# Spreading the block transfers of a head's transposition over eight steps in a two-layer decoder kernel

## The chip, the cores and the metric

The kernel runs on one core of a Trainium2 chip. The metric is the time of one execution on the device in microseconds (us); lower is better. The core has five engines that run side by side and wait for each other through semaphores: TensorE (PE in the rows, its weight loads PEld), VectorE (DVE), ScalarE (ACT), GpSimd (POOL) and SyncE (SP), which here only issues DMA transfers. Each engine works through its own list of instructions in order.

## The reference

The input x has 256 positions of 2048 numbers. Two layers follow, each with a norm, one wide projection, a mixer over 32 heads of 128, a gate and a projection back.

```
def even_layer(x, norm_g, w_in, q_gain, k_gain, w_out):
    hdn = rms_norm(x, norm_g)
    proj = jnp.einsum('bsd,de->bse', hdn, w_in)
    qa, ka, va, qb, kb, vb, gate = split_cols(
        proj, [D_SB, D_SB, D_SB, D_DIL, D_DIL, D_DIL, D_INNER])
    oa = stick_breaking_attention(to_heads(qa), to_heads(ka), to_heads(va))
    ob = dilated_attention(to_heads(qb), to_heads(kb), to_heads(vb), q_gain, k_gain)
    mix = jnp.concatenate([oa.reshape(b, s_len, D_SB), ob.reshape(b, s_len, D_DIL)], axis=-1)
    mix = mix * jax.nn.silu(gate.astype(jnp.float32))
    return x + jnp.einsum('bse,ed->bsd', mix.astype(x.dtype), w_out)

def odd_layer(x, norm_g, w_in, lb, o_gain, w_out):
    hdn = rms_norm(x, norm_g)
    proj = jnp.einsum('bsd,de->bse', hdn, w_in)
    q, f_pre, inp, gate = split_cols(proj, [D_INNER, D_INNER, D_INNER, D_INNER])
    o = hgrn2(to_heads(q), to_heads(f_pre), to_heads(inp), lb)
    o = rms_norm(o, o_gain).reshape(b, s_len, D_INNER)
    mix = o * jax.nn.silu(gate.astype(jnp.float32))
    return x + jnp.einsum('bse,ed->bsd', mix.astype(x.dtype), w_out)
```

Heads 0 to 15 of the first layer are stick-breaking attention, heads 16 to 31 a mixture of three dilated causal softmax attentions, and the 32 heads of the second layer are HGRN2, a gated linear recurrence.

## The kernel before

**Steps.** The wide projection runs head by head: 16 *steps* a head, each one block of 128 input channels times 512 columns (128 each of q, k or forget gate, v, and gate). A step is six matmuls of 128x512 (`product`, lines 277 to 279): the single-precision product is made from a rounded part and a rest of each factor, hi x hi, hi x lo and lo x hi, for two halves of the sequence. Each layer ends with an output projection of 4 x 32 such steps. All in all there are 1280 steps.

**Weights.** `Feed` brings in 512 KB for two steps at a time: a load on SP's queue (L223, tile `raw`, four buffers), a rounding copy on ACT (L234, `whi`) and a subtraction on DVE (L235, `wlo`), together called a *split* here. `take` keeps four splits ahead, and `whi` and `wlo` have four buffers each, so the split for a pair of steps can only begin when PE has finished the pair four pairs before.

**Side work.** When a head's 16 steps are done, its generator (`head`) is added to `Side`. After every step of what follows, `tick` advances each generator whose count has run out; `yield n` means that the rest is written n steps later. So the work of head h is written between the matmuls of the next heads: `evacuate` (L300) copies q and k into `qkp` and v and gate into `pj`, then comes the gate, the transposition of q and k (`turn_pair`), the products (L336, L337 for attention; L487 and after for HGRN2), the softmax or its like, its transposition (`flip_weights`, L137), the product with the values (L327 to L329), and the mix, which is transposed again (`emit_mix`, L137) and split for the output projection. The order in which the instructions of each engine finally stand is set by a list scheduler of the framework, which may move work by a part of a step or a few.

**The transposition.** VectorE can transpose blocks of 32x32 only, so the blocks are first carried to their places by 16 DMA transfers of 16 KB, all on SP's queue (`move_blocks`, L148, from `qkp` to `mvp`). `yield 4` later one DVE instruction turns them in place (`turn_blocks`, L155). The last head of a layer is transposed on PE instead (`quick`). SP's queue also carries all weight loads.

**The three kinds.** Stick-breaking: transfers 2 steps after the evacuation, turn 4 later, products 3 later. Dilated: transfers 5 after the evacuation, since q and k need their norms first, turn 4 later together with a scaling of k on ACT (L385), products 3 later. HGRN2: transfers 2 after, turn 4 later, then a chain of some 20 small DVE operations from the forget gate (L431 to L480, most of them recorded under the helper's line L439), and 10 steps later the first scores on PE (L487): two matmuls from tile `sp`, then two that read `qv`, the last tile of that chain.

Of the kernel before, what the change touches and what calls it, by code (L numbers as in the profile page):

```python
# [10 lines left out]
F32 = mybir.dt.float32  # L11
# [7 lines left out]
P = 128  # L19
D = 2048  # L20
SEQ = 256
NT = SEQ // P
NKT = D // P
NH = 32
# [4 lines left out]
LB_FLOOR = 2.0 ** -28  # L29
GATE_FLOOR = -87.0  # L30
AHEAD = 4


@with_exitstack
def hybrid_trunk(
# [21 lines left out]
    work = ctx.enter_context(tc.tile_pool(name="work", bufs=3))  # L57
# [27 lines left out]
    def constants():  # L85

        nc.sync.dma_start(ident, eye)
        nc.sync.dma_start(strict, cmask[:, 2, :])
        nc.sync.dma_start(bias, cmask[:, 0, :])
        nc.sync.dma_start(hg, headg)  # L90
        nc.sync.dma_start(lbr, lbl)
        nc.sync.dma_start(mult, cmask[:, 1, :])
        hmf = work.tile([P, 4, 80], F32, name="pj", bufs=2)
        nc.sync.dma_start(hmf, hmask)
        yield 1
        nc.vector.scalar_tensor_tensor(
            qkg, hg[:, 0:1], 1.0 / math.sqrt(P), hg[:, 1:2], op0=ALU.mult, op1=ALU.mult
        )
        yield 1
        for t in range(NT):  # L100
            nc.vector.tensor_copy(hm[:, 4 * t : 4 * t + 4, :], hmf)

        nc.vector.tensor_max(lbm, lbr[:, 0, :], lbr[:, 1, :])
        for j in range(2):
            nc.vector.tensor_sub(lbe[:, j, :], lbr[:, j, :], lbm)
        nc.scalar.activation(lbe, lbe, AF.Exp)
        nc.vector.tensor_add(lbs, lbe[:, 0, :], lbe[:, 1, :])
        nc.vector.reciprocal(lbs, lbs)
        nc.vector.tensor_mul(lb, lbe[:, 1, :], lbs)
        nc.vector.tensor_scalar(oml, lb, -1.0, 1.0, op0=ALU.mult, op1=ALU.add)  # L110
        nc.vector.tensor_scalar_max(lbc, lb, LB_FLOOR)
# [21 lines left out]
    def flip(blocks):  # L133

        ps = psb.tile([P, len(blocks) * P], F32, name="att")
        for i, b in enumerate(blocks):
            nc.tensor.transpose(ps[:, i * P : (i + 1) * P], b, ident)  # L137
        return ps

    def move_blocks(src, name):  # L140

        n = src.shape[2] // P
        moved = work.tile([P, NT, n, 4, 32], F32, name=name, bufs=1)
        to = moved.rearrange("p t c a j -> p (t c) a j")
        v = src.rearrange("p t (c f) -> p (t c) f", f=P)
        for a in range(4):
            for b in range(4):
                nc.sync.dma_start(  # L148
                    to[32 * b : 32 * b + 32, :, a, :], v[32 * a : 32 * a + 32, :, 32 * b : 32 * b + 32]
                )  # L150
        return moved

    def turn_blocks(dst, moved):

        nc.vector.transpose(dst, moved.rearrange("p t c a j -> p (t c a j)"))  # L155

    def turn_pair(qk, quick):


        if quick:  # L160
            ps = flip([qk[:, t, c * P : (c + 1) * P] for t in range(NT) for c in range(2)])
            nc.scalar.copy(qk, ps.rearrange("p (t f) -> p t f", t=NT))
        else:
            moved = move_blocks(qk, "mvp")
            yield 4
            turn_blocks(qk.rearrange("p t f -> p (t f)"), moved)

    def flip_weights(w):

        ps = flip([w[:, j * P : (j + 1) * P] for j in range(3)])  # L170
        at = work.tile([P, 384], F32, name="atk", bufs=2)
        nc.scalar.copy(at, ps)
        return at
# [37 lines left out]
    class Feed:  # L211
# [26 lines left out]
        def take(self):  # L238
            while len(self.parts) < AHEAD:
                n = len(self.parts)  # L240
                self.split()
                if len(self.parts) == n:
                    break
            return self.parts.pop(0)
# [49 lines left out]

    def evacuate(acc, rstd):
        qk = work.tile([P, NT, 256], F32, name="qkp", bufs=2)
        vg = work.tile([P, NT, 256], F32, name="pj", bufs=2)
        for dst, c in ((qk, 0), (vg, 256)):
            for t in range(NT):
                nc.scalar.activation(  # L300
                    dst[:, t, :], acc[t][:, c : c + 256], AF.Copy, scale=rstd[:, t : t + 1]
                )
        return qk, vg

    def gate_exp(vg):

        g = vg[:, :, P:]
        sg = work.tile([P, NT, P], F32, name="sg")
        nc.vector.tensor_scalar(sg, g, GATE_FLOOR, -1.0, op0=ALU.max, op1=ALU.mult)
        nc.scalar.activation(sg, sg, AF.Exp)  # L310
        nc.vector.tensor_scalar_add(sg, sg, 1.0)
        nc.vector.reciprocal(sg, sg)  # L312
        nc.vector.tensor_mul(sg, sg, g)
        return sg
# [3 lines left out]
    def emit_mix(h, mix, scale):  # L318
        mixed.append(h)
        split_into(mixh[:, h, :], mixl[:, h, :], flip([mix[:, t, :] for t in range(NT)]), scale)  # L320
# [18 lines left out]

    def stick_breaking(h, qk, vg):  # L340
        sg = gate_exp(vg)
        yield 2
        yield from turn_pair(qk, False)
        yield 3
        zp = products(qk)
        z = work.tile([P, 384], F32, name="wt", bufs=2)
        nc.vector.scalar_tensor_tensor(
            z, zp, 1.0 / math.sqrt(P), strict, op0=ALU.mult, op1=ALU.add
        )
        sp = work.tile([P, 384], F32, name="qv", bufs=2)  # L350
        nc.scalar.activation(sp, z, AF.Abs)
        nc.scalar.activation(sp, sp, AF.Exp, scale=-1.0)
        nc.scalar.activation(sp, sp, AF.Ln, bias=1.0)
        nc.vector.scalar_tensor_tensor(sp, z, 0.0, sp, op0=ALU.max, op1=ALU.add)

        for lo, hi in ((0, 128), (128, 384)):
            back = sp[:, lo:hi][:, ::-1]
            nc.vector.tensor_tensor_scan(back, one.broadcast_to([P, hi - lo]), back, 0.0, ALU.mult, ALU.add)
        nc.vector.tensor_sub(z, z, sp)
        nc.scalar.activation(z, z, AF.Exp)  # L360
        yield 12
        at = flip_weights(z)
        yield 3
        o = weighted_values(at[:, 0:128], at[:, 128:256], at[:, 256:384], vg)
        nc.vector.tensor_mul(sg, o, sg)
        yield 2
        emit_mix(h, sg, 1.0)

    def dilated(h, qk, vg):
        sg = gate_exp(vg)  # L370
# [8 lines left out]
        for t in range(NT):  # L379
            sl = qk[:, t, P:]  # L380
            nc.vector.tensor_scalar_mul(sl, sl, rr[:, 2 * t + 1 : 2 * t + 2])
        yield 5
        yield from turn_pair(qk, h == NH - 1)
        k = qk[:, :, P:]
        nc.scalar.activation(k, k, AF.Copy, scale=qkg)  # L385
        yield 3
        z = products(qk)
        nm = small.tile([P, NT], F32, name="nm")
        ws = small.tile([P, NT], F32, name="ws")
# [30 lines left out]

    def hgrn(h, qk, vg):
        g = vg[:, :, P:]
        sg = work.tile([P, NT, P], F32, name="sg")
        nc.scalar.activation(sg, g, AF.Sigmoid)
        nc.vector.tensor_mul(sg, sg, g)
        yield 2
        yield from turn_pair(qk, h == NH - 1)
        q, fp = qk[:, :, 0:P], qk[:, :, P:]
        fk = work.tile([P, 2, SEQ], F32, name="qk", bufs=2)
# [188 lines left out]
    for layer in range(2):  # L618
        for h in range(NH):
            acc = accumulators()  # L620
            steps = product(feed, xh, xl, NKT, acc, layer)
            for k in range(NKT):
# [4 lines left out]
                if layer == 0 and h == 0 and k % 4 == 3:  # L627
                    n = k // 4
# [98 lines left out]
```

## Time and profile before

| what | value |
|---|---|
| time, median of 3 runs | 1991.98 us (1991.17 to 1992.28) |
| the profiled execution | 1995.66 us, its span 1993.9 us |
| PE busy | 1945.4 us, 98% of the span |
| DVE busy, ACT busy | 1319.1 us (66%), 1010.2 us (51%) |
| granted clock of TensorE, mean | 0.999 |
| DMA moved | 360.79 MB, 181 GB/s |

The span reaches from the first to the last instruction of the profiled execution. A row of a timeline gives start, duration, engine, line, operation and tiles, and in brackets the time that the engine sat idle before it with the instruction that ended the wait. A matmul's shown duration overlaps that of the next one, so the distance of two starts is what one costs when they follow each other. SPq is SP's queue of DMA issues: its durations are those of issuing, not of the transfer.

### The profile page before, as it was taken

How to read it: one execution, taken by the hardware profiler on the slowest of the kernel's cores; microseconds unless marked ns; L12 is line 12 of the kernel's file. 1: busy time of each engine (PE TensorE's matmuls, PEld its weight loads, DVE VectorE, ACT ScalarE, POOL GpSimd, SP SyncE). 2: the span in 40 equal slices, each digit the busy share in tenths (PEclk: the TensorE clock that was granted, in tenths of full speed). 3: DMA queues.
4: the chain of work that ended last, by engine and by line, in shares of the span. 5: the costliest groups of instructions: out<-in, count | busy, mean ns of one | idle time of the engine just before them, and what ended most of it. 6: DMA issues, size and time to landing. Idle time of an engine off the chain costs nothing.

```text
span 1993.9 us, 26825 instructions
## 1 busy us (share of the span) xinstructions
PE 1945.4 (98%) x9032; PEld 1587.2 (80%) x9032; DVE 1319.1 (66%) x2518; ACT 1010.2 (51%) x1719; POOL 53.3 (3%) x54
## 2 busy tenths in 40 slices
PE   8999999999999999999999999999999999999999
PEld 7778877877777777888877778787877777778887
DVE  6666666666666666555557777777777777777443
ACT  6455555544444444444455555555555555555432
POOL 0000000000000000000000000000000000000000
PEclk9999999999999999999999999999999999999999
DMA  8566655655555555665555555555556555565664
GB/s 304 164 199 194 186 180 181 189 169 181 166 171 182 182 168 177 201 190 190 189 168 172 179 178 177 168 171 169 171 178 180 171 165 169 172 178 171 200 201 138
DMA packets 240267, 360.79 MB, mean 181 GB/s; under 512 B 153984, under 2 KB 155136, under 8 KB 240128
## 3 DMA queue, kind: packets, MB, share of 16 engines
q1 hardware_dynamic: 239984, 359.05, 57.9%
q8 instruction: 71, 1.16, 0.2%
q14 instruction: 68, 0.56, 0.1%
q10 hardware_dynamic: 144, 0.02, 0.0%
HBM read 340.61 MB, written 2.10 MB: 172 GB/s over the span
## 4 chain that ended last, share of the span: by engine, by line
PE 55%; DVE 18%; SPq 10%; issue 7%; ACT 5%; DMA 4%; POOL 1%; DVEq 0%; ACTq 0%; POOLq 0%
PE acc L277 17%; PE acc L279 17%; PE acc L278 17%; SPq L148 10%; DVE wlo L235 5%; ACT whi L234 4%; DMA raw<-in_w_even 2%; DVE qk L439 2%; DVE ri L455 2%; PE att L487 1%; DMA mvp<-qkp 1%; PE att L516 1%; POOL ro L202 1%; DVE sg L312 1%; DVE wt L469 1%
## 5 line engine op out<-in xcount | busy, mean ns | idle before, releaser
L235 DVE TENSOR_TENSOR wlo<-raw,whi 128x1024 fp32r<-128x1024 f32 (+1 forms) x642 | 781.3, 1218 | 447.6 <-ACT whi L234 447.1
L234 ACT CAST whi<-raw 128x1024 fp32r<-128x1024 f32 (+1 forms) x642 | 672.3, 1048 | 786.2 <-PE acc L279 654.6
L277 PE MATMUL acc<-whi,xh 128*128 128x512 f32 x2048 | 829.6, 405 | 6.1 <-ACT whi L234 6.1
L278 PE MATMUL acc<-wlo,xh 128*128 128x512 f32 x2048 | 803.9, 393 | 0.6 <-DVE wlo L235 0.6
L279 PE MATMUL acc<-whi,xl 128*128 128x512 f32 x2048 | 802.9, 392 | 0.0
L279 PEld LDWEIGHTS acc<-whi,xl 128*128 128x128 f32 x2048 | 385.5, 188 | 83.7
L277 PEld LDWEIGHTS acc<-whi,xh 128*128 128x128 f32 x2048 | 385.9, 188 | 81.8 <-ACT whi L234 6.1
L278 PEld LDWEIGHTS acc<-wlo,xh 128*128 128x128 f32 x2048 | 386.4, 189 | 74.9 <-DVE wlo L235 1.8
L277 PE MATMUL acc<-whi,mixh 128*128 128x512 f32 x512 | 202.0, 394 | 0.0
L279 PE MATMUL acc<-whi,mixl 128*128 128x512 f32 x512 | 199.5, 390 | 0.0
L278 PE MATMUL acc<-wlo,mixh 128*128 128x512 f32 x512 | 199.4, 390 | 0.0
L279 PEld LDWEIGHTS acc<-whi,mixl 128*128 128x128 f32 x512 | 96.1, 188 | 20.0
L277 PEld LDWEIGHTS acc<-whi,mixh 128*128 128x128 f32 x512 | 96.1, 188 | 19.6
L278 PEld LDWEIGHTS acc<-wlo,mixh 128*128 128x128 f32 x512 | 96.2, 188 | 19.3
L155 DVE STREAM_TRANSPOSE qkp<-mvp 128x512 f32<-128x512 f32 x62 | 44.1, 711 | 49.7 <-DMA mvp<-qkp 49.6
L300 ACT ACTIVATE qkp<-acc,rstd 128x256 f32<-128x256 f32 x128 | 60.4, 474 | 12.3 <-PE acc L279 9.3
L300 ACT ACTIVATE pj<-acc,rstd 128x256 f32<-128x256 f32 x128 | 60.2, 472 | 0.0
L312 DVE RECIPROCAL sg<-sg 128x256 f32<-128x256 f32 x32 | 56.0, 1749 | 0.5
L202 POOL TENSOR_TENSOR rr<-rv,mhalf 128x4 f32<-128x4 f32 x16 | 29.4, 1839 | 736.5 <-DVE rv L201 736.5
L439 DVE TENSOR_TENSOR qk<-qk,tots 128x128 f32<-128x128 f32 x64 | 18.5, 288 | 43.0 <-PE att L516 42.9
L202 POOL TENSOR_TENSOR ro<-rv,mhalf 128x2 f32<-128x2 f32 x32 | 22.3, 697 | 839.0 <-DVE rv L201 839.0
L558 DVE SCALAR_TENSOR_TENSOR sg<-att,ro,sg 128x128 f32<-128x128 f32 x64 | 22.1, 349 | 27.8 <-POOL ro L202 27.8
(137 smaller groups left out, 1261.1 us busy)
## 6 DMA issues: line engine op xcount, KB each, us to landing
raw<-in_w_odd SPq DMA_DIRECT2D x256, 512.0 KB, 4.6
raw<-in_w_even SPq DMA_DIRECT2D x254, 512.0 KB, 4.2
raw<-in_w_out SPq DMA_DIRECT2D x128, 512.0 KB, 3.5
mvp<-qkp SPq DMA_DIRECT2D x992, 16.0 KB, 2.1
xres<-in_xt SPq DMA_DIRECT2D x8, 256.0 KB, 6.5
xres<-in_x SPq DMA_DIRECT2D x4, 512.0 KB, 8.0
out<-xres SPq DMA_DIRECT2D x6, 256.0 KB, 5.0
raw<-in_w_even SPq DMA_DIRECT2D x4, 256.0 KB, 4.3
```

Source lines behind the costliest of these rows:

```text
L148: nc.sync.dma_start(to[32 * b : 32 * b + 32, :, a, :], v[32 * a : 32 * a + 32, :, 32 * b : 32 * b + 32])
L155: nc.vector.transpose(dst, moved.rearrange("p t c a j -> p (t c a j)"))
L202: nc.gpsimd.tensor_tensor(dst, v[:, 0:n], mhalf[:, 0:n], op=ALU.pow)
L234: nc.scalar.copy(hi[:, s, :], half[:, s, :])
L235: nc.vector.tensor_sub(lo[:, s, :], half[:, s, :], hi[:, s, :].bitcast(F32))
L277: nc.tensor.matmul(acc[t], sh[:, k, s], hi, start=(k == 0), stop=False)
L278: nc.tensor.matmul(acc[t], sh[:, k, s], lo, start=False, stop=False)
L279: nc.tensor.matmul(acc[t], sl[:, k, s], hi, start=False, stop=(k == nk - 1))
L300: nc.scalar.activation(dst[:, t, :], acc[t][:, c : c + 256], AF.Copy, scale=rstd[:, t : t + 1])
L312: nc.vector.reciprocal(sg, sg)
L439: nc.vector.tensor_tensor(o, a, b.broadcast_to(list(o.shape)), op=ALU.mult)
L455: nc.vector.reciprocal(ri, f8[:, :, 3:8])
```

## The change

Each head's sixteen block transfers are written two at a time, one pair after each of eight successive steps, in place of all at once. Because the generator yields between the pairs, the weight loads of those steps stand between them on SP's queue. The turn is written 4 steps after the last pair, and whatever follows it moves along: counted from the evacuation, the turn comes at 13 steps in place of 6 (stick-breaking and HGRN2) and at 15 in place of 9 (dilated). The distance from the turn to the products is 4 steps in place of 3 for stick-breaking and 5 in place of 3 for dilated heads (the scaling of k is now one step behind the turn); in HGRN2 the chain starts one step behind the turn, and from its start to the first scores there are 10 steps as before. The tile `pj` (values and gates) gets three buffers in place of two and the tile `sg` four in place of three, as they are held longer.

```
-    def move_blocks(src, name):
-        n = src.shape[2] // P
-        moved = work.tile([P, NT, n, 4, 32], F32, name=name, bufs=1)
+    def move_blocks(moved, src):
         to = moved.rearrange("p t c a j -> p (t c) a j")
         v = src.rearrange("p t (c f) -> p (t c) f", f=P)
         for a in range(4):
...
                     to[32 * b : 32 * b + 32, :, a, :], v[32 * a : 32 * a + 32, :, 32 * b : 32 * b + 32]
                 )
-        return moved
+                if b % 2:
+                    yield 1
...
-            moved = move_blocks(qk, "mvp")
-            yield 4
+            moved = work.tile([P, NT, 2, 4, 32], F32, name="mvp", bufs=1)
+            yield 2
+            yield from move_blocks(moved, qk)
+            yield 3
             turn_blocks(qk.rearrange("p t f -> p (t f)"), moved)
+            yield 1
...
-        vg = work.tile([P, NT, 256], F32, name="pj", bufs=2)
+        vg = work.tile([P, NT, 256], F32, name="pj", bufs=3)
...
-        sg = work.tile([P, NT, P], F32, name="sg")
+        sg = work.tile([P, NT, P], F32, name="sg", bufs=SG)
...
         sg = gate_exp(vg)
-        yield 2
         yield from turn_pair(qk, False)
         yield 3
         zp = products(qk)
...
-        yield 5
+        yield 5 if h == NH - 1 else 2
         yield from turn_pair(qk, h == NH - 1)
         k = qk[:, :, P:]
         nc.scalar.activation(k, k, AF.Copy, scale=qkg)
-        yield 3
+        yield 4
         z = products(qk)
...
-        yield 2
+        if h == NH - 1:
+            yield 3
         yield from turn_pair(qk, h == NH - 1)
```

`SG` is 4. Lines behind the changed places stand up to four lower, so L223, L235, L336 and L487 of before are L227, L239, L340 and L491 in the changed kernel.

The first place is SP's queue in the steady stretch of the stick-breaking heads, one head's worth, before (`raw` are weight loads, `mvp` block transfers):

```order
L148 DMA mvp<-qkp 32x4x32 x2
L223 DMA raw<-in_w_even 128x1024
L148 DMA mvp<-qkp 32x4x32 x5
L223 DMA raw<-in_w_even 128x1024
L148 DMA mvp<-qkp 32x4x32 x9
L223 DMA raw<-in_w_even 128x1024 x6
```

And the same in the changed kernel:

```order
L148 DMA mvp<-qkp 32x4x32 x2
L227 DMA raw<-in_w_even 128x1024
L148 DMA mvp<-qkp 32x4x32 x7
L227 DMA raw<-in_w_even 128x1024
L148 DMA mvp<-qkp 32x4x32 x2
L227 DMA raw<-in_w_even 128x1024
L148 DMA mvp<-qkp 32x4x32
L227 DMA raw<-in_w_even 128x1024
L148 DMA mvp<-qkp 32x4x32 x2
L227 DMA raw<-in_w_even 128x1024
L148 DMA mvp<-qkp 32x4x32 x2
L227 DMA raw<-in_w_even 128x1024 x3
```

The sixteen transfers stood among two loads; now they stand among five, and the last pair has a load directly ahead of it.

The second place is DVE around the turn of a dilated head, before (the rows under L393 belong to the products of the same head; `wlo` rows are splits):

```order
L235 TENSOR_TENSOR wlo<-raw,whi 128x1024 x2
L129 SCALAR_TENSOR_TENSOR mixl<-att,mixh 128x256
L235 TENSOR_TENSOR wlo<-raw,whi 128x1024
L155 STREAM_TRANSPOSE qkp<-mvp 128x512
L393 ISA sp,nm<-att,bias 128x128
L393 ISA nm 128x1
L393 ISA sp,nm<-att,bias 128x256
L393 ISA nm 128x1
L235 TENSOR_TENSOR wlo<-raw,whi 128x1024
```

And in the changed kernel (L313 to L384 are the gate and the norms of the next head):

```order
L239 TENSOR_TENSOR wlo<-raw,whi 128x1024
L156 STREAM_TRANSPOSE qkp<-mvp 128x512
L313 TENSOR_SCALAR sg<-pj 128x256
L376 TENSOR_TENSOR sp<-qkp 128x512
L378 TENSOR_REDUCE s_4761<-sp 128x4
L315 TENSOR_SCALAR sg<-sg 128x256
L205 TENSOR_SCALAR rv<-s_4761 128x4
L130 SCALAR_TENSOR_TENSOR mixl<-att,mixh 128x256
L316 RECIPROCAL sg<-sg 128x256
L384 TENSOR_SCALAR qkp<-qkp,rr 128x128
L317 TENSOR_TENSOR sg<-sg,pj 128x256
L384 TENSOR_SCALAR qkp<-qkp,rr 128x128
```

Before, the products' reduction followed directly on the turn; now two splits stand between them, and the turn is the first of eleven side operations that stand between two splits.

The third place is PE at the first scores of an HGRN2 head, before (in brackets the engines whose semaphores the instruction waits for):

```order
L487 MATMUL att<-sp 128x128 [waits DVE_49,PE_49,Activation_49]
L487 MATMUL att<-sp 128x128
L487 MATMUL att<-qv,qk 128x192 [waits DVE_49,Activation_49]
L487 MATMUL att<-qv,qk 128x192
L277 MATMUL acc<-whi,xh 128x512
```

And in the changed kernel:

```order
L491 MATMUL att<-sp 128x128 [waits PE_49]
L491 MATMUL att<-sp 128x128
L491 MATMUL att<-qv,qk 128x192 [waits Activation_49]
L491 MATMUL att<-qv,qk 128x192
L281 MATMUL acc<-whi,xh 128x512
```

The scores now carry no wait for DVE of their own: an earlier wait of PE covers it. Counted in PE's order, in steps from the end of the head's own sixteen, the products stand at 10.5 before and 18 after in stick-breaking heads, at 14.7 and 21 in dilated heads, and the first scores at 17 and 25 in HGRN2 heads. The turn stands two splits later on DVE in all three kinds.

## Rows read from the trace of the kernel before

**Rows 1.** Page, span and busy time, share and instructions of each engine

```profile
span 1993.9 us, 26825 instructions
...
PE 1945.4 (98%) x9032; PEld 1587.2 (80%) x9032; DVE 1319.1 (66%) x2518; ACT 1010.2 (51%) x1719; POOL 53.3 (3%) x54
```

**Rows 2.** Whom PE waited for: total us, times, longest

```profile
PE att L336 <- ACT qkp L385: 18.2, 15, 2.0
PE att L487 <- DVE pr L500: 12.4, 31, 1.0
...
PE att L336 <- DVE qkp L155: 5.2, 6, 2.2
```

**Rows 3.** Busy us per engine, dilated heads, then HGRN2 heads

```profile
431.00:820.00 389.00, 370.76 (x1719) 303.31 (x1718) 255.00 (x483) 188.34 (x279) 27.51 (x15) 1.00 0.56 178
1020.00:1815.00 795.00, 781.99 (x3729) 633.15 (x3727) 590.37 (x1448) 430.94 (x890) 20.92 (x30) 1.00 0.58 174
```

**Rows 4.** SP queue, timeline around the transfers of one dilated head

```profile
609.00 1.89 SPq L148 DMA_DIRECT2D mvp<-qkp  x3
610.99 0.53 SPq L223 DMA_DIRECT2D raw<-in_w_even  x1
611.56 8.32 SPq L148 DMA_DIRECT2D mvp<-qkp  x13
```

**Rows 5.** DVE, the turn of that head

```profile
621.22 0.71 DVE L155 STREAM_TRANSPOSE qkp<-mvp 128x512 f32<-128x512 f32 x1 [0.54 <-DMA mvp<-qkp]
```

**Rows 6.** ACT, scaling of k in that head

```profile
621.97 0.51 ACT L385 ACTIVATE qkp<-qkp,qkg 128x256 f32<-128x256 f32 x1 [2.55 <-DVE qkp L155]
```

**Rows 7.** PE, ahead of the products of that head

```profile
621.57 0.39 PE L277 MATMUL acc<-whi,xh 128*128 128x512 f32 x1
622.53 0.49 PE L336 MATMUL att<-qkp 128*128 128x128 f32 x2 [0.57 <-ACT qkp L385]
```

**Rows 8.** PE, first scores of one HGRN2 head

```profile
1419.15 0.39 PE L279 MATMUL acc<-whi,xl 128*128 128x512 f32 x1
1419.38 0.60 PE L487 MATMUL att<-sp 128*128 128x128 f32 x4
1420.36 0.89 PE L487 MATMUL att<-qv,qk 128*128 128x192 f32 x4 [0.38 <-DVE pr L500]
```

**Rows 9.** DVE, end of the chain of that head

```profile
1419.41 0.28 DVE L439 TENSOR_TENSOR qv<-wt,tots 128x128 f32<-128x128 f32 x1
1419.61 0.47 DVE L129 SCALAR_TENSOR_TENSOR mixl<-att,hg,mixh 128x256 fp32r<-128x256 f32 x1
1420.00 0.21 DVE L439 TENSOR_TENSOR qv<-qv,tots 128x64 f32<-128x64 f32 x1
```

**Rows 10.** Whom DVE waited for

```profile
DVE qkp L155 <- DMA mvp<-qkp: 49.6, 52, 5.3
```

**Rows 11.** Page, costliest groups: count, busy us, mean ns, idle before

```profile
L234 ACT CAST whi<-raw 128x1024 fp32r<-128x1024 f32 (+1 forms) x642 | 672.3, 1048 | 786.2 <-PE acc L279 654.6
...
L300 ACT ACTIVATE qkp<-acc,rstd 128x256 f32<-128x256 f32 x128 | 60.4, 474 | 12.3 <-PE acc L279 9.3
...
L312 DVE RECIPROCAL sg<-sg 128x256 f32<-128x256 f32 x32 | 56.0, 1749 | 0.5
```

**Rows 12.** Issues under L148: min/median/max ns, and time to landing

```profile
L148 SPq DMA_DIRECT2D mvp<-qkp x992: 585/599/1706, 44.0 to 1795.2; - x199
...
DMA to landing us min/median/max: 1.8/2.1/6.7
```

**Rows 13.** Landing of transfers to mvp, 1408 to 1434 us

```profile
DMA to landing us min/median/max: 1.8/3.4/5.4
```

**Rows 14.** DVE, gate and norms of one dilated head

```profile
501.25 0.29 DVE L309 TENSOR_SCALAR sg<-pj 128x256 f32<-128x256 f32 x1
...
503.11 1.22 DVE L235 TENSOR_TENSOR wlo<-raw,whi 128x1024 fp32r<-128x1024 f32 x1
...
506.56 1.22 DVE L235 TENSOR_TENSOR wlo<-raw,whi 128x1024 fp32r<-128x1024 f32 x1
```

More of the change, by code (lines that the diff above doesn't have):

```diff
@@ L31 @@
 AHEAD = 4
+SG = 4
 @with_exitstack
@@ L92, in constants @@
         nc.sync.dma_start(mult, cmask[:, 1, :])
-        hmf = work.tile([P, 4, 80], F32, name="pj", bufs=2)
+        hmf = work.tile([P, 4, 80], F32, name="pj", bufs=3)
         nc.sync.dma_start(hmf, hmask)
@@ L422, in hgrn @@
         g = vg[:, :, P:]
-        sg = work.tile([P, NT, P], F32, name="sg")
+        sg = work.tile([P, NT, P], F32, name="sg", bufs=SG)
         nc.scalar.activation(sg, g, AF.Sigmoid)
         nc.vector.tensor_mul(sg, sg, g)
-        yield 2
+        if h == NH - 1:
+            yield 3
         yield from turn_pair(qk, h == NH - 1)
```

## The prediction

> **What bounds the kernel now.** I read the page first: PE is busy 1945.4 of 1993.9 us [rows 1], so at most 48.5 us of idle PE can be won by reordering; all else is matmuls, which the change neither adds nor removes. The second view is whom PE waited for [rows 2]. Three lines hold nearly all of it after the start: the products at L336 waited 18.2 us for ACT's scaling of k (15 dilated heads) and 5.2 us for DVE's turn (6 stick-breaking heads), and the scores at L487 waited 12.4 us for DVE (31 HGRN2 heads). The windows agree: over the dilated heads PE is idle 389.0 - 370.8 = 18.2 us, over the HGRN2 heads 795.0 - 782.0 = 13.0 us [rows 3]. Weights are not among these lines: SP's sixteen issues in a row do hold back loads, but four splits ahead cover that.
>
> Third, the timeline behind each wait. In a dilated head SP issues the transfers from 609.00 to 619.88, sixteen at 0.6 us with one load between [rows 4, 12]. The turn, next in line on DVE, waits for the last landing until 621.22 [rows 5]; ACT, which stood 2.55 us idle for the turn, scales k at 621.97 [rows 6]; PE's products start at 622.53, after 0.57 us of idleness [rows 7]. So the path is 10.9 us of issuing, some 1.3 of landing, then turn and scaling, and the four steps (5.4 us) that the source leaves for the transfers are too few. In an HGRN2 head the first two scores start at 1419.38, but `qv`, the last tile of the chain, is written at 1420.00 to 1420.21, and the second two start at 1420.36 [rows 8, 9]; the record names the operation behind it. The chain starts with the turn, so it is late for the same reason, or is simply too long for its ten steps; both are answered by more steps.
>
> **What a wait costs.** A stop costs more than the idle time shown, since a matmul's shown 0.39 us overlaps its successor: matmuls follow at 0.23 us (1419.15 to 1419.38 [rows 8]), but the products start 0.96 us after the matmul ahead [rows 7]. That is 0.73 us lost for 0.57 shown, 0.16 more. For the products: 23.4 us shown in 21 stops, plus 21 x 0.16 = 3.4, makes 26.8 us. For the scores: the first two are four instructions in 0.60 us, each shown as about 0.27, so their starts lie 0.11 apart and the last is at 1419.71; the next starts 0.65 us later, 0.54 more than 0.11. Times 31, 16.7 us. Together 43.5 us can be won.
>
> **The change part by part.** *Issues.* No DMA is added: sixteen issues of 0.6 us a head stay, and eight loads. In the stretch where pairs and loads alternate SP has, for two steps (2 x 6 x 0.23 = 2.7 us), four issues of 0.6 and a load of up to 0.53, 2.9 us in all. It falls back by 0.2 us per two steps, 0.8 us in eight, and catches up in the other eight. I take it as free; if it were not, it would show in the next item.
>
> *When the last pair lands.* The last pair now stands behind a load, which itself waits until a split has freed its buffer: by the order, the split two before the turn in stick-breaking and HGRN2 heads, three before it in dilated ones. Splits are paced by PE, ACT being idle 654.6 us until PE gives a buffer back [rows 11], so two of them are 5.4 us or more. In these the load (0.53), two issues (1.2) and the landing must fit. A landing takes 2.1 us in the median [rows 12], but 3.4 us where transfers are mixed with loads [rows 13], and 6.7 at most. With 3.4 the sum is 5.1 us: the turn waits for nothing, or a few tenths. With 6.7 it is 8.4, and the turn waits 3.0 us. I take 3.4, since the window with that median is the one where loads stand between. The rule that speaks against the change is in the Trainium skill, "DMA: Bandwidth & Descriptors", section "Queues, rings and completion order": each DMA engine takes the descriptors of one ring in order, so a small transfer behind a 512 KB load on SP's queue waits for the load's bytes. The longer landing in the mixed window agrees with it.
>
> *The slack from the turn on.* The turn moves by two splits, four steps, on DVE; the products move by 7.5 steps in stick-breaking, 6.3 in dilated, the scores by 8 in HGRN2 heads (counted in the order). What is gained between turn and consumer is thus 3.5, 2.3 and 4 steps of 1.36 us: 4.8, 3.2 and 5.4 us. What was missing was at most 2.2, 2.0 and 1.0 us [rows 2]. Even the longest wait of 3.0 us for a landing would be covered in stick-breaking and HGRN2 heads (4.8 - 2.2, 5.4 - 1.0 leave 2.6 and 4.4, and those shortages contained such waits already); in dilated heads the last pair has one split more. So all three waits go: 43.5 us. The order says the same in its way: products and scores no longer stand inside a step, and the scores have no wait for DVE left.
>
> *What is no longer held.* DVE's 49.6 us of waiting for landings [rows 10] and ACT's waits behind it go too. Both have slack, so that alone is worth nothing. The third `pj` and fourth `sg` buffer are needed because values and gate now live past the second evacuation that follows; they add no instruction.
>
> *What moves with it.* All side matmuls shift together, so their distances within a head stay, and none waits that did not. At both layer ends the last two heads come closer together, and the last is turned on PE: there and in the first three heads I leave 1.5 us of waits. The gain is 42 us.
>
> **The sum.** 1993.9 - 42 = 1951.9 us of span. The profiled execution was 1995.66, 3.7 us above the median 1991.98, which stands for the same work, so the time is 1991.98 - 42 = **1950 us**.
>
> **The rivals.** *First, the turn stays late in part of the heads.* If transfers behind loads land at 6.7 us and SP's backlog adds 0.8, the turn waits 3.8 us. That takes most of the slack in the two kinds with two splits; dilated heads, where k's scaling comes after the turn in ACT's order behind four evacuations of 0.47 us [rows 11], could keep their 18.2 us + 15 x 0.16 = 20.6. Gain 43.5 - 20.6 = 23: 1969 us. For it speaks that every transfer is now near a load; against it that the order gives dilated heads three splits.
>
> *Second, slower: the splits become late.* In dilated heads the turn now heads a run of eleven side operations on DVE with no split between. Before, these took from 501.25 to 506.56, less one split of 1.22: 4.1 us [rows 14], with 1.75 of them the reciprocal [rows 11]; add the turn's 0.71 and 0.47 for the mix [rows 5, 9], and the run is 5.3 us. Count from the moment that PE frees the buffer of the split ahead of the run: 2.3 us for that split (1.05 on ACT, 1.22 on DVE), 1.0 for two evacuations ahead of it on ACT, 5.3 for the run, 1.2 for the next split, 9.8 in all. PE needs that next split four pairs of steps later, after 4 x 2.7 = 10.9 us and the side matmuls between. The margin is 1.1 us, and about 2 with those matmuls, an estimate. If the turn waits for its transfers, the wait is added in front of the run. To turn a gain of 43 us into a loss, PE would have to stand 43.5 / 15 = 2.9 us more in each of 15 dilated heads, so the turn would have to wait 4.9 us each time. The longest wait of any turn was 5.3 us, in the start [rows 10], the mean 49.6 / 52 = 1.0. At 6 us of waiting the kernel would take 1992 + 15 x 1.1 = 2008 us.
>
> *Third, no change: the waits move on.* The products stop waiting but the next PE group of the head does (the transposed weights, the values, the mix). Then the time stays at 1992. Against it: these groups keep their distance from the products or scores, and none waited for more than tenths before, although the products themselves were late.
>
> **How the numbers follow.** Full gain, 0.75, with a range of its own from 1944 (all 48.5 us of idleness, which includes the start) to 1957 (a fifth kept). Partial gain, 0.15, from 1957 to 1985. No change, 0.04. Slower, 0.06. The range from 1943 to 1972 takes in the first and the middle of the second. 0.2% of this kernel is 4 us, about what a measurement can tell from no change; faster by more than that is 0.90, within it 0.04, slower 0.06.
>
> **What would show it.** In the profile after: PE busy share near 99.5%, and no line of L340 or L491 above 2 us among PE's waits; DVE's waits of the turn for DMA under 20 us in place of 49.6; the median landing of block transfers up from 2.1 to 3 us or more, without effect. If the first rival holds, L340 still waits for ACT's scaling, 15 times. If the second holds, PE waits at L282 for `wlo`, once per dilated head. The prediction is wrong if PE's idleness shows up under another line, or if the distance of matmuls without any wait (0.23 us) grows.

## The result, and the profile after

The changed kernel takes 1939.25 us in the median of four runs (1938.98 to 1939.30), beside 1992.13 us for the kernel before (four runs, 1991.17 to 1993.06): a ratio of 0.9734, with a 95% interval from 0.9717 to 0.9751. That is 52.9 us less. The forecast was 1950 us with a range from 1943 to 1972: the direction held, the size did not, and the time lies under the range.

The page of the changed kernel, span and busy time (against [rows 1]):

```profile
span 1937.5 us, 26795 instructions
...
PE 1928.2 (100%) x9032; PEld 1586.1 (82%) x9032; DVE 1322.8 (68%) x2518; ACT 1026.4 (53%) x1719; POOL 69.4 (4%) x54
```

The span fell by 56.4 us (the execution profiled of before had been 3.7 us above its median, that of after is not). PE's idle time fell from 48.5 to 9.3 us, 39.2. The other 17.2 us came out of PE's *busy* time, although it executes the same 9032 matmuls. This is what the forecast had not reckoned with.

Whom PE waited for, the only line left, and it is the kernel's start (against [rows 2]):

```profile
PE acc L281 <- ACT whi L238: 5.6, 1, 5.6
```

The windows over the dilated and the HGRN2 heads, PE's busy time in the second column (against [rows 3]):

```profile
419.00:799.00 380.00, 380.00 (x1782) 315.74 (x1781) 262.05 (x489) 194.33 (x286) 15.12 (x15) 1.00 0.59 189
997.00:1772.00 775.00, 775.00 (x3732) 631.18 (x3731) 597.23 (x1459) 441.01 (x886) 50.27 (x30) 1.00 0.55 177
```

There is no idle time in either. SP's queue around the transfers of one dilated head (against [rows 4]):

```profile
582.22 1.88 SPq L148 DMA_DIRECT2D mvp<-qkp  x3
584.15 1.06 SPq L227 DMA_DIRECT2D raw<-in_w_even  x2
585.25 0.59 SPq L148 DMA_DIRECT2D mvp<-qkp  x1
586.90 0.33 SPq L227 DMA_DIRECT2D raw<-in_w_even  x1
587.28 2.52 SPq L148 DMA_DIRECT2D mvp<-qkp  x4
590.21 0.34 SPq L227 DMA_DIRECT2D raw<-in_w_even  x1
590.59 2.52 SPq L148 DMA_DIRECT2D mvp<-qkp  x4
593.21 0.53 SPq L227 DMA_DIRECT2D raw<-in_w_even  x1
593.79 2.52 SPq L148 DMA_DIRECT2D mvp<-qkp  x4
```

From 587.28 on the queue hardly rests, but every load goes out between two groups of four transfers. The last issue ends at 596.31. DVE's timeline of the turn and of the run of side work behind it (against [rows 5, 14]):

```profile
600.82 0.70 DVE L156 STREAM_TRANSPOSE qkp<-mvp 128x512 f32<-128x512 f32 x1
...
603.54 1.74 DVE L316 RECIPROCAL sg<-sg 128x256 f32<-128x256 f32 x1
...
605.86 1.22 DVE L239 TENSOR_TENSOR wlo<-raw,whi 128x1024 fp32r<-128x1024 f32 x1
```

The turn waits for nothing: it stands 4.5 us behind the last issue. The run behind it lasts 5.0 us, and the split that follows is no cause of a wait on PE. PE at the products of that head (against [rows 7]), and at the first scores of an HGRN2 head (against [rows 8]):

```profile
605.84 0.39 PE L283 MATMUL acc<-whi,xl 128*128 128x512 f32 x1
606.07 0.38 PE L340 MATMUL att<-qkp 128*128 128x128 f32 x2
...
1383.79 0.39 PE L283 MATMUL acc<-whi,xl 128*128 128x512 f32 x1
1384.02 0.60 PE L491 MATMUL att<-sp 128*128 128x128 f32 x4
1384.47 0.82 PE L491 MATMUL att<-qv,qk 128*128 128x192 f32 x4
```

The products start 0.23 us after the matmul ahead, where before it was 0.96; the second pair of scores starts 0.45 us after the first, where before it was 0.98. Whom DVE waited for: of 49.6 us of waiting for landings [rows 10] this is left:

```profile
DVE qkp L156 <- DMA mvp<-qkp: 0.6, 1, 0.6
```

The time from issue to landing of these transfers, a little longer in the median than in [rows 12]:

```profile
DMA to landing us min/median/max: 1.8/2.7/6.8
```

### The profile page after: what moved, and what is told of

It reads as the page before. It is cut to its first block, busy times and chain, and to the rows that moved or that the text cites. A ratio compares the mean times of both kernels' runs of the same rounds, so it can differ in the third digit from the quotient of the medians.

```text
span 1937.5 us, 26795 instructions
## 1 busy us (share of the span) xinstructions
PE 1928.2 (100%) x9032; PEld 1586.1 (82%) x9032; DVE 1322.8 (68%) x2518; ACT 1026.4 (53%) x1719; POOL 69.4 (4%) x54
## 4 chain that ended last, share of the span: by engine, by line
PE 100%; DMA 0%; ACT 0%; DVE 0%; DVEq 0%; issue 0%
PE acc L281 31%; PE acc L283 30%; PE acc L282 30%; PE att L491 2%; PE att L138 1%; PE att L520 1%; PE att L332 1%; PE att L333 1%; PE att L331 1%; PE att L341 1%; PE att L340 0%; PE att L548 0%; DMA gn<-in_gains 0%; ACT xh L129 0%; ACT whi L238 0%; DVE xres L594 0%
## 5 line engine op out<-in xcount | busy, mean ns | idle before, releaser
L239 DVE TENSOR_TENSOR wlo<-raw,whi 128x1024 fp32r<-128x1024 f32 (+1 forms) x642 | 781.6, 1219 | 473.6 <-ACT whi L238 470.9
L281 PE MATMUL acc<-whi,xh 128*128 128x512 f32 x2048 | 831.5, 406 | 5.6 <-ACT whi L238 5.6
L282 PE MATMUL acc<-wlo,xh 128*128 128x512 f32 x2048 | 800.2, 391 | 0.0
L281 PEld LDWEIGHTS acc<-whi,xh 128*128 128x128 f32 x2048 | 385.5, 188 | 81.1 <-ACT whi L238 5.6
L282 PEld LDWEIGHTS acc<-wlo,xh 128*128 128x128 f32 x2048 | 386.0, 188 | 74.0 <-DVE wlo L239 0.9
L281 PE MATMUL acc<-whi,mixh 128*128 128x512 f32 x512 | 202.6, 396 | 0.0
L282 PE MATMUL acc<-wlo,mixh 128*128 128x512 f32 x512 | 199.3, 389 | 0.0
L282 PEld LDWEIGHTS acc<-wlo,mixh 128*128 128x128 f32 x512 | 96.2, 188 | 19.3
L281 PEld LDWEIGHTS acc<-whi,mixh 128*128 128x128 f32 x512 | 96.2, 188 | 19.3
L206 POOL TENSOR_TENSOR ro<-rv,mhalf 128x2 f32<-128x2 f32 x32 | 51.7, 1615 | 789.8 <-DVE rv L205 789.8
L206 POOL TENSOR_TENSOR rr<-rv,mhalf 128x4 f32<-128x4 f32 x16 | 16.1, 1008 | 711.7 <-DVE rv L205 711.7
L534 ACT COPY ri<-qk 128x128 f32<-128x128 f32 x32 | 9.6, 299 | 59.2 <-DVE qk L443 59.0
L435 ACT ACTIVATE qk<-qkp 128x256 f32<-128x256 f32 x32 | 13.3, 417 | 47.9 <-DVE qkp L156 47.9
```

The source lines that it names most:

```text
L206: nc.gpsimd.tensor_tensor(dst, v[:, 0:n], mhalf[:, 0:n], op=ALU.pow)
L239: nc.vector.tensor_sub(lo[:, s, :], half[:, s, :], hi[:, s, :].bitcast(F32))
L281: nc.tensor.matmul(acc[t], sh[:, k, s], hi, start=(k == 0), stop=False)
L282: nc.tensor.matmul(acc[t], sh[:, k, s], lo, start=False, stop=False)
```

## The experiments

Two theories of why the waits went. *Room*: what counts is that the turn and its consumers are written later, and the transfers could go out at once. *Spreading*: what counts is that SP's queue no longer holds loads back behind sixteen issues. A third, the two extra buffers, was to be excluded. The kernel before, run beside each group of experiments, had medians of 1994.05, 1993.62 and 1995.23 us; the ratios are to these, the differences in us to the changed kernel's 1939.25.

**All sixteen at once, everything else where the change puts it.**

```
-                if b % 2:
-                    yield 1
+                if a == 3 and b == 3:
+                    yield 8
```

> All sixteen block transfers of a head are issued in one go again, at the step of the first pair; the turn and all that follows stay where the change puts them, and the buffers too. Theory 1 (the gain is the room between the transfers, the turn and PE's products, and how the transfers are issued does not matter): within 4 us of the changed kernel's 1939 us, no wait of PE above 1 us after the start. Theory 2 (the pairs between the loads are what helps, because a run of sixteen issues holds back the weight loads): over 1960 us, with waits of PE for whi or wlo.

1957.52 us (1956.27 to 1958.87), ratio 0.9817 [0.9803, 0.9832]: between the two expectations, 18.3 us above the changed kernel. Whom PE waited for:

```profile
PE att L138 <- DVE sg L415: 11.1, 11, 1.8
PE acc L281 <- ACT whi L238: 6.4, 2, 5.8
```

Neither products nor scores wait any more: for them room alone is enough, although DVE's turn still waits 54.8 us in all for landings, more than before the change. Stick-breaking and HGRN2 heads last 23.76 and 25.35 us from one to the next in the median, as in the changed kernel. Nearly all of the loss is in dilated heads, at the mix (L138), a group that never waited before: 16.5 of the 19.2 us in its trace, by the distances of starts, explained below. The rest is mostly in the first stick-breaking heads, with one wait of 1.3 us for ACT's transposed weights and one of 0.6 us for `whi`. The timelines of SP, DVE, ACT and PE in one dilated head:

```profile
598.41 8.32 SPq L148 DMA_DIRECT2D mvp<-qkp  x13
606.83 1.97 SPq L227 DMA_DIRECT2D raw<-in_w_even  x4
...
608.08 0.71 DVE L156 STREAM_TRANSPOSE qkp<-mvp 128x512 f32<-128x512 f32 x1 [2.64 <-DMA mvp<-qkp]
612.04 1.23 DVE L239 TENSOR_TENSOR wlo<-raw,whi 128x1024 fp32r<-128x1024 f32 x1 [3.25 <-ACT whi L238]
613.18 0.60 DVE L415 SCALAR_TENSOR_TENSOR sg<-att,ws,sg 128x128 f32<-128x128 f32 x2
...
608.83 0.51 ACT L388 ACTIVATE qkp<-qkp,qkg 128x256 f32<-128x256 f32 x1 [3.57 <-DVE qkp L156]
610.96 1.05 ACT L238 CAST whi<-raw 128x1024 fp32r<-128x1024 f32 x1 [1.62 <-DMA raw<-in_w_even]
...
613.58 0.59 PE L138 MATMUL att<-ident,sg 128*128 128x128 f32 x2 [1.29 <-DVE sg L415]
```

Thirteen issues in a row hold four loads back until 606.83. DVE, in order, stands at the turn until 608.08; then ACT's rounding waits for the held load, DVE's split waits for ACT until 612.04, and the multiplication that PE's mix needs (L415) is queued behind that split. In the dilated heads the held loads never reach PE as missing weights; they reach it through the order of two other engines. All eleven stops at the mix show this pattern: the split ahead of L415 had waited 3.0 to 3.2 us for ACT, and ACT's rounding 1.3 to 1.6 us for a load.

**The pairs spread, but the turn one step behind the last pair and its consumers at the distance of before.**

```
             yield from move_blocks(moved, qk)
-            yield 3
             turn_blocks(qk.rearrange("p t f -> p (t f)"), moved)
-            yield 1
...
-        yield 4
+        yield 3
         z = products(qk)
```

> The transfers go out two in a step as in the change, but the turn follows one step behind the last pair, and products and scores keep the distance from the turn that they had before (three steps, three steps, ten steps). Theory 1 (room): the last pair cannot have landed when the turn is due, DVE waits for it in most heads, over 40 us in total, and PE's products wait again: 1960 to 1995 us. Theory 2 (spreading): the transfers are no longer late, 1939 to 1945 us.

1955.47 us (1954.93 to 1956.41), ratio 0.9807 [0.9793, 0.9822]: again between the two, 16.2 us above the changed kernel. Whom PE waited for:

```profile
PE att L338 <- ACT qkp L386: 4.8, 12, 1.1
PE att L489 <- DVE pr L502: 0.6, 2, 0.3
```

DVE's turn waits 56.7 us in all for landings. Spreading without room leaves the products of the dilated heads waiting for the scaling of k, as in [rows 2] but with 4.8 us in place of 18.2. (By the distances of starts, explained below, the loss at the products is 12.3 us and at the second scores 2.8.) So each half of the change brings about two thirds of the gain, 36.5 and 38.6 us of the 54.8 that lie between the changed kernel and the 1994.05 us beside these two, and only both bring it all: room for products and scores, spreading for the loads behind the transfers. The halves are not quite clean: eight pairs take eight steps, so the turn of the second kernel still stands three to four steps later than before, and both kernels have the extra buffers, whose share the next runs show.

**The two extra buffers alone, in the kernel before.**

```
-        vg = work.tile([P, NT, 256], F32, name="pj", bufs=2)
+        vg = work.tile([P, NT, 256], F32, name="pj", bufs=3)
...
-        sg = work.tile([P, NT, P], F32, name="sg")
+        sg = work.tile([P, NT, P], F32, name="sg", bufs=4)
```

> The kernel before, with three buffers for values and gates and four for the gate's tile, nothing else. Theories 1 and 2: no change, 1988 to 1996 us. A third theory (the same short idleness of PE in every HGRN2 head is a lack of buffers): 1970 to 1980 us, the scores' wait of 12.4 us being gone.

1990.1 us (1988.13 to 1992.24), ratio 0.998 [0.9971, 0.999]: inside the first expectation, but 3.95 us less than the kernel before beside it, and by the interval 2 to 6 us. The waits stay:

```profile
PE att L336 <- ACT qkp L385: 16.3, 15, 1.9
PE att L487 <- DVE pr L500: 12.7, 31, 1.0
```

**The changed kernel without them** (`pj` with two buffers, `SG = 3`).

> The changed kernel with two buffers of values and gates and three of the gate's product, as before; the transfers and all steps stand where the change puts them. The evacuation of a head, 32 steps behind that of two heads earlier, now has to wait until the weighted values of that head are through (32, 31 and 33 steps behind its evacuation in the three kinds). If the third buffer is what lets the later turn stand, evacuations wait on ACT for PE by up to a step or two, splits are held behind them and PE shows waits for ACT or for the turn: 1945 to 1965 us. If the held ACT work is covered by the splits made four ahead, it is 1939 to 1943 us.

1939.09 us (1938.73 to 1939.32), ratio 0.9721 [0.9708, 0.9734], where the changed kernel itself ran beside it, as a control:

> The changed kernel itself, beside the two others of this call: 1939 us, within 1.

It took 1939.37 us (1939.11 to 1939.43), ratio 0.9722 [0.9709, 0.9735]. The buffers are worth nothing in the changed kernel. The evacuation does wait for the values of two heads earlier, 15 times, but on ACT, which has time for it:

```profile
ACT pj L304 <- PE att L333: 8.7, 15, 0.6
```

**One kind of head at a time back on the schedule of before.** In each of three kernels, `turn_pair` gets a branch with the old order (all transfers, four steps, the turn), and one kind of head uses it with its old distances; for stick-breaking heads:

```
+            if once:
+                for _ in move_blocks(moved, qk):
+                    pass
+                yield 4
+                turn_blocks(qk.rearrange("p t f -> p (t f)"), moved)
+                return
...
         sg = gate_exp(vg)
-        yield from turn_pair(qk, False)
+        yield 2
+        yield from turn_pair(qk, False, True)
```

> The changed kernel, with the sixteen stick-breaking heads on the schedule of before (all transfers at once, turn and products early). It measures what that kind's waits cost. If a stop of PE costs the idle time that is shown and 0.16 us more, as predicted: 5.2 us shown in 6 stops make 6.2, so 1945.5 us. If a stop costs more, and the small stops in the first heads count too (the trace of before against that of after has 14 us between them over these heads): 1950 to 1955 us.

> The changed kernel with only the dilated heads back on the schedule of before. By the prediction's rule (idle time of the products in rows 2, 18.2 us in 15 waits, and 0.16 us more for each) it is 20.6 us slower than the changed kernel, 1960 us. By the theory that a stop also slows the matmuls behind it (from the distances of starts in the two traces, where a dilated head before took 0.8 to 2.2 us longer than after, about 22.4 us in the stretch) it is 1961 to 1962 us. By the theory that the three kinds lean on each other (a late head of one kind delays the next kind's), the losses of the three runs of this sort would not add up to the 52.9 us between before and after.

> The changed kernel with only the HGRN2 heads back on the schedule of before. By the prediction's rule (31 waits of 0.38 us and 0.16 us more for each, 16.7 us) it is 1956 us. By the theory that a stop also slows the next matmuls of its group (2.3 us from the starts behind the 31 stops) and that the first head adds waits of its own (1.1 us) it is 1959 us. With 11.35 us of the stick-breaking run and the dilated run beside it, the sum should be 52.9 us within about 3 if the three kinds are independent.

Measured: stick-breaking 1950.6 us (1949.63 to 1950.98, ratio 0.9782 [0.9767, 0.9796]), dilated 1960.13 us (1959.14 to 1961.03, 0.9834 [0.9818, 0.985]), HGRN2 1957.8 us (1957.46 to 1958.01, 0.9821 [0.9806, 0.9835]). The losses are 11.35, 20.9 and 18.55 us. For each, the main line of whom PE waited for (one from each kernel, in this order):

```profile
PE att L346 <- DVE qkp L156: 5.2, 6, 2.3
```

```profile
PE att L346 <- ACT qkp L394: 15.5, 14, 1.8
```

```profile
PE att L496 <- DVE pr L509: 11.8, 31, 0.7
```

Each loss is 5 to 7 us more than the idle time shown. To see where it sits I took the distance from each matmul's start to the next one's, summed by what follows what, and subtracted the same sum of the changed kernel (blank: under 0.2 us):

```
us more than in the changed kernel      stick  dilated  HGRN2  before
first products, from the matmul ahead    7.55    17.80           28.59
next matmuls of the same products        0.82     1.61            2.50
second scores, from the first scores                     15.86   16.51
next matmuls of the second scores                         2.27    2.26
128x512 after 128x512                    1.47     0.20   -0.99    2.50
all other                                1.39     0.15    1.23    3.13
all                                     11.23    19.76   18.37   55.49
```

A stop shows in three places: as idle time, as the end of the matmul ahead that no longer overlaps its successor, and in the next matmuls of the stopped group, which also come later (2.27 us behind 31 stops, 0.07 each). The last two are counted as busy. The three losses add up to 50.8 of the 52.9 us, so the kinds hardly lean on each other. 2.1 us are left, or 3.6 to 4.0 against the 1994.05 and 1993.62 us of the kernel before beside these runs. The buffers are the likely part: the three kernels have them, alone they took 2 to 6 us off the kernel before, and in that run the distance to the first products came out at 25.83 us in this measure, against 28.59, and 7.55 + 17.80 = 25.35. The clock is another: 1.6 of the 2.50 us under "128x512 after 128x512" in the last column come from one stretch at 1.2 GHz (last section), which none of these three traces has. No run separates the two.

**Fewer groups of side matmuls.** In the changed kernel a 128x512 matmul follows another after 0.227 us, but the first one behind a group of side matmuls takes 0.315 us to its successor (medians), and the next few a little more than 0.227. If that were the price of a group, joining groups should pay. So in two kernels later matmuls of a head were moved to steps in which the next head has matmuls anyway; the full version:

```
         at = flip_weights(z)
-        yield 3
+        yield 4
...
         nc.vector.tensor_mul(sg, o, sg)
-        yield 2
+        yield 12
...
         at = flip_weights(pr)
-        yield 3
+        yield 16 if h < NH - 2 else 3
...
-        yield 2
+        yield 8 if h < NH - 2 else 2
         emit_mix(h, sg, 1.0)
...
         decay(64, tot)
-        yield 2
+        yield 11 if h < NH - 2 else 2
...
         nc.scalar.copy(cross, px)
-        yield 2
+        yield 3 if h < NH - 2 else 2
...
-        yield 2
+        yield 9 if h < NH - 2 else 2
         emit_mix(h, sg, hg[:, 2:3])
```

> The changed kernel, but later matmuls of a head are put into the step in which the next head's come anyway: stick-breaking weighted values with the next products and the mix with the next flip, the same in dilated heads with the flip and the products, and in HGRN2 the last score block and the mix with the next head's first scores and the values with the first halves. No matmul is added or taken away; about 156 of some 400 groups of side matmuls vanish as groups of their own. In the trace of the changed kernel the matmuls of 128x512 behind a group lose 0.11 to 0.21 us together against their 0.227 us. If that is a cost for each group, this kernel is about 20 us faster than the changed kernel, 1915 to 1925 us. If it is a cost of each side matmul, or of the data it reads, it stays at 1939 us. If the joined work waits for results or for free PSUM buffers (four of them, up to four groups in one step), it is slower and waits of the side matmuls for DVE or ACT appear.

> As the run with joined groups, but with one join a head: stick-breaking values with the next products, the dilated mix with the next products, the HGRN2 mix with the next scores; 60 groups vanish. A cost for each group gives about 8 us, 1931 us; a cost of each side matmul gives 1939 us; at most three groups stand in one step, so that waits for PSUM buffers should not come.

> The kernel with joined groups again, beside the changed kernel: 1934 us. If its 5 us below the changed kernel are real and not a difference of two chips, the intervals of the two ratios do not overlap here.

The full version took 1934.12 us (1933.8 to 1934.28, ratio 0.9702 [0.9687, 0.9716]), the mild one 1937.25 us (1937.05 to 1937.46, 0.9718 [0.9703, 0.9732]). Run again beside the changed kernel, the full one took 1933.99 us (1933.84 to 1934.35, 0.9696 [0.9683, 0.9709]). The intervals of those two ratios overlap, since the kernel before scatters over 3 us; the runs themselves do not come near each other (1934.35 at most against 1939.11 at least), so it beats both kernels by a clear if small 5.4 us over the changed one. But only about a quarter of what a cost for each group promised came: the groups fall from 327 to 271 and 183 in the traces, and 5.1 us for 144 of them is 0.035 us each. PE in one HGRN2 head of the full version, where three jobs meet:

```profile
1379.07 0.39 PE L283 MATMUL acc<-whi,xl 128*128 128x512 f32 x1
1379.30 0.38 PE L138 MATMUL att<-ident,sg 128*128 128x128 f32 x2
1379.52 0.39 PE L548 MATMUL att<-wt,qk 128*128 128x128 f32 x2
1379.74 0.61 PE L491 MATMUL att<-sp 128*128 128x128 f32 x4
1380.19 0.82 PE L491 MATMUL att<-qv,qk 128*128 128x192 f32 x4
```

They follow without a pause and nothing new waits, so the third outcome in the expectation falls. Most of the cost thus goes with the side matmuls themselves, and joining does not take it away. The traces show why: most of what the 0.315 us have over 0.227 is time of the group's own last matmul, booked late (last section).

## Why the prediction was right and wrong

**Right.** The waits: the first products waited for the scaling of k and for the turn, and the second scores for DVE; all three waits are gone and none took their place. That SP's backlog is no loss, that the last pair lands in time and that the turn waits under 20 us in all (0.6) held. The median landing rose from 2.1 to 2.7 us, in the direction of the rule that the prediction cites from the Trainium skill, though not to the 3 us named. PE's busy share came out at 1928.2 / 1937.5 = 99.5%, as forecast, and the distance of matmuls without a wait stayed 0.227 us.

**The rivals.** The second one's run of side work is there (5.0 us against 5.3 reckoned), but with the turn on time its margin holds. The third one, waits that move on to the mix, did not happen here; it is exactly what happens where the transfers go out at once. That also answers a premise of the prediction, that four splits ahead cover the loads which sixteen issues hold back, so that the gain is all slack: with the slack alone 18.3 us stay lost to the held loads. The forecast did not suffer, since the change does both. The first one's late turn in dilated heads is what the kernel with an early turn shows.

**Wrong: the size, 42 us against 52.9.** The term for the dilated products came out right (20.6 against 20.9 measured), in part by luck: the kernel measured shows 15.5 us of idleness in 14 stops, which the prediction's rule makes 17.7 us; its first products start 17.80 us late, and 1.61 us lie in the next matmuls, which the rule leaves out. These were mis-sized:

- "For the products ... 21 stops, plus 21 x 0.16": for stick-breaking heads that made 5.2 + 6 x 0.16 = 6.2 us, and the run says 11.35. The profile lists six waits, but the starts ahead of the products are 7.55 us late, and 3.7 us lie in other places: matmuls behind the stops and small waits of other groups, which I had not counted.
- The scores: 16.7 against 18.55. The distance to the second pair was right (15.86 to 16.51); the 2.27 us behind it, and 1.1 us in the first HGRN2 head, were left out.
- "I leave 1.5 us of waits" at the layer ends: none came.
- The buffers "add no instruction", so nothing, and the clock does not stand in the sum at all. The 2.1 us left over are likely these two: the buffers alone took 2 to 6 us off the kernel before, though they are worth nothing in the changed kernel, where I had even called them needed; and a stretch at 1.2 GHz costs 1.6 us in the profile of before.

5.15 + 1.85 + 1.5 = 8.5 us are shown of the 10.9 that were missing; the dilated term gives 0.3, and 2.1 are only what is left over.

The step that failed ahead of these is the first of all: "at most 48.5 us of idle PE can be won by reordering; all else is matmuls". It fixed the lower end of the range at 1943. PE's busy time is not a fixed amount of work here: a matmul is shown with 0.39 us while its successor starts after 0.23, so at each stop the overlap is lost and the loss is booked as busy (and so are the 1.6 us of matmuls at the lower clock). I had seen this for a single stop (the 0.16 us) and not drawn the consequence for the bound. The Trainium skill, "Perfetto Trace Analysis", section "Identifying the Most-Contended Engine", says of TensorE's busy share that it is no good measure of how near a kernel is to its limit, since matmuls are pipelined, and names the share of weight loads as one of two to use instead. This trace agrees: PEld's busy time stayed (1587.2 and 1586.1 us) while PE's fell by 17.2.

## What to carry to other kernels

Where matmuls are pipelined, size a stop by the distances of starts, up to the end of the stopped group, against the same distances in a head that does not stop; PE's idle time is no ceiling of what can be won: in each of the three kernels with one kind of head put back it was 5 to 7 us less than the loss. When many small transfers share an in-order queue with bulk loads, give the consumer more steps *and* let the loads through between them: held loads may show up at an instruction that never waited, queued on another engine behind the work that the load feeds. If a change brings buffers with it, run it without them too.

## What the runs showed of the hardware beyond that

The first 128x512 matmul behind a group of side matmuls takes 0.315 us to the next start, against 0.227 (327 groups in the changed kernel; 0.336 us in 182 groups of the joined one). Summed over all 128x512 matmuls that follow one another, the distances exceed 0.227 us by about 46 us in the changed kernel (7352 at a mean of 0.2332), 34.8 of them at these first ones. That looks like the largest loss left, but 20.7 of the 46 us are none. The changed kernel at the end of the scores shown above:

```profile
1384.47 0.82 PE L491 MATMUL att<-qv,qk 128*128 128x192 f32 x4
1384.98 0.53 PE L281 MATMUL acc<-whi,xh 128*128 128x512 f32 x1
1385.35 0.40 PE L282 MATMUL acc<-wlo,xh 128*128 128x512 f32 x1
```

These four scores start 0.163 us apart, but the last stands only 0.028 us ahead of L281, which then takes 0.37. Four times 0.163 and once 0.227 lead from 1384.47 to 1385.35, where L282 starts: nothing is lost, the last score's time is booked at its successor. So at a change from small to large matmuls one distance of starts is not the cost of one matmul; the two have to be taken together. Taken so, the 264 groups that end in matmuls of 128 to 256 columns cost 1.5 us in all beyond what the same matmuls take elsewhere. Only the 63 that end in 64-column matmuls (L520) do cost more, 12.7 us, 0.20 each. With 10.6 us at the next eight matmuls, about 25 of the 46 us are a loss. Joining took away groups of the first sort: the excess at the group ends fell from 14.1 to 13.4 us, that at the next eight matmuls from 10.6 to 6.8. Why the 64-column groups cost more was not settled: no run changed the type or the operands of the side matmuls.

The granted clock was 1.00 in the windows over dilated and HGRN2 heads, before as after, but the stops did meet a lower clock elsewhere. In the profile of before it fell to 0.50 (1.2 in place of 2.4 GHz) from 125.07 to 128.48 us, 1.4 us after PE had stood idle for 2.20 us. PE's timeline, and a window inside that stretch (the granted clock is the third number from the right):

```profile
123.69 0.46 PE L336 MATMUL att<-qkp 128*128 128x128 f32 x2 [2.20 <-DVE qkp L155]
...
126.41 0.63 PE L278 MATMUL acc<-wlo,xh 128*128 128x512 f32 x1
126.84 0.63 PE L279 MATMUL acc<-whi,xl 128*128 128x512 f32 x1
...
125.20:128.40 3.20, 3.20 (x9) 2.52 (x8) 1.56 (x2) 2.79 (x5) 0.00 (x0) 0.50 1.01 413
```

Matmuls of 128x512 follow one another there after 0.427 us in place of 0.227, and eight of them lose 1.6 us, all booked as busy. The run with the buffers alone has such a stretch of 3.41 us too, right behind a stop of 1.95 us; the run with the stick-breaking heads put back has a stop of 2.27 us and no such stretch. The changed kernel has none before its last 1.5 us.

The kernel without stops also repeats itself far better: its runs lie between 1938.98 and 1939.43 us in all groups, at a mean granted clock of 1.000 in all nine; those of the kernel before beside the experiments lie between 1990.73 and 1997.02, at 0.997 to 1.000. The medians of these 29 runs go with the clock: 1993.0 us at 1.000, 1994.0 at 0.999, 1995.0 at 0.998 and 1995.9 at 0.997. So a part of the scatter goes with the clock; whether the landing of transfers, which the stops wait for, has a part too was not tested.
